# Final norm of the tokens spread over the last experts, and rows of the last three experts normed by themselves

## The chip, the cores and the metric

The kernel runs on one core of a Trainium2 chip. The metric is the device time of one execution in microseconds (us); for a kernel it is the median of several runs. A profile is one further execution, taken by the hardware profiler. Engines are named as in the profile: PE (matmul), PEld (its weight load), DVE (vector), ACT (scalar), POOL (GpSimd), SP (the queue that issues most DMAs).

## The reference

One layer over 1024 latent tokens of width 1024 and 256 context tokens: a token mixer, then a mixture of experts, then a final norm. What matters here is the end:

```python
def rmsnorm(x, g):
    y = x * lax.rsqrt(jnp.mean(x * x, axis=-1, keepdims=True) + EPS)
    return y * g

def expert_choice_ffn(h, w_r, w1, w3, w2):        # 16 experts, D 1024, F 2048
    cap = EC_FACTOR * n // N_EXPERTS               # 128 tokens for each expert
    aff = jax.nn.softmax(h @ w_r, axis=-1)
    gate, idx = lax.top_k(jnp.swapaxes(aff, 1, 2), cap)
    xe = h[bidx, idx]
    hid = jax.nn.silu(xe @ w1) * (xe @ w3)
    ye = (hid @ w2) * gate[..., None]
    return jnp.zeros_like(h).at[bidx, idx].add(ye)

x = x + g2x * expert_choice_ffn(hx2, w_router, w1, w3, w2)
return rmsnorm(x, final_g)
```

An expert chooses its 128 tokens, so a token may be chosen by several experts or by none, and a row of the output can be normed for good only when every expert that chose it has added its part. All data are fp32.

## The kernel before

The mixer, the second norm and the router take the time to about 480 us. They leave two arrays in DRAM: `hx2d`, the normed tokens that the experts gather from, and `x2d`, the residual stream that they add to. From there on the loop over 16 experts runs.

**One expert.** Its weights are 24 units of 1 MB, each 128 x 2048 fp32: eight of w1 and eight of w3 (up) and eight of w2 (down). SP loads them (`load_next`, L91) into a ring of 12 slots with the tag `raw`. A unit is split before use: ACT copies it rounded into `hi` (L107), DVE subtracts, `lo = raw - hi` (L109); three `hi`/`lo` pairs are held. PE then makes three passes over a unit (hi x hi, lo x hi, hi x lo: L1257, L1259, L1261 for up, L1300, L1303, L1306 for down). A slot of the ring comes free when DVE has made `lo`.

**Routing.** `route_oh(e)` makes on DVE a one-hot block `oh` (L1218) from the positions of the router. `route(e)` multiplies it on PE into the token numbers `ix` and the gates `gate` (L1226 to L1230) and gathers the expert's rows `xe` from `hx2d` with an indirect DMA that POOL issues (L1235). `transpose_x(e)` turns `xe` into its `hi` and `lo`. `oh` and `xe` share a tag `xe` with two buffers.

**Order.** Instructions run on each engine in the order in which the program writes them. The loop is software-pipelined by hand: iteration e runs `up("3", e)`, with `transpose_x(e+1)` behind its unit 2, `route_oh(e+2)` behind unit 3 and `route(e+2)` behind unit 6; then `hidden(e)` (DVE, L1278: the product of silu and the second up product, four pieces `sg`); `up("1", e+1)` with `transpose_h(e)` in it; and `down(e)` with the silu of expert e+1 in it (ACT, L1268). The last two iterations are in another order: up 3 of 14, up 1 of 15, silu, up 3 of 15, down of 14, down of 15.

**End of an expert.** At the end of `down(e)` DVE makes `ye`, the product of the PSUM result, the gate and the row `g2row` (L1313, two halves of 512), and POOL issues an indirect DMA that adds the 128 rows of `ye` into `x2d` (L1316, the scatter-add). `ye` has a buffer of its own in the pool `mb`.

**The end before.** Expert 15 has no scatter-add. SP reads `x2d` back in four pieces `xf` (L1384) once the scatter-add of expert 14 has landed. `ye` of expert 15 is split into `yh` and `yl` and spread by matmuls with the one-hot block `ohT` (L1374; L1403 to L1405) over the eight token tiles. For each tile: the sum (`residual`, DVE L1412, or within PSUM), Square and Sqrt on ACT (L1422, L1427), reciprocal on DVE (L1439), the product with the gain row `fg` (DVE L1446, or POOL L1434 and DVE L1444), and an output DMA by SP (L1447).

Of the kernel before, what the change touches and what calls it, by code (L numbers as in the profile page):

```python
# [45 lines left out]
def hybrid_layer(ctx, tc, x, c, ctxt, c_ctx, w_mod, b_mod, norm1_g, norm2_g, w_in, sgu_g, sgu_w,  # L46
# [36 lines left out]

    def load_next(n=1, queue=nc.sync):
        for _ in range(n):
# [1136 lines left out]
    def route(e):  # L1222
# [8 lines left out]
        if e == NE - 1:  # L1231
            V.tensor_copy(ixf, p[:, 0:1])
# [148 lines left out]
    xf = [raw2([P, 4, D], F32, "xf") for _ in range(2)]  # L1381
    fs = mp.tile([P, 3, 8], F32, name="fs")
    for q in range(4):
        nc.sync.dma_start(xf[q // 2][:, q % 2 * 2:q % 2 * 2 + 2],  # L1384
                          x2d[q * 256:(q + 1) * 256].rearrange("(t p) d -> p t d", p=P))
    ye = down(NE - 1)
    yh = mb.tile([P, D], F32R, name="yh", tag="xth")
    yl = mb.tile([P, D], F32R, name="yl", tag="xtl")
    for n in range(2):
# [1 line left out]
        A.activation(yh[:, sl], ye[:, sl], AF.Copy)
        V.tensor_sub(yl[:, sl], ye[:, sl], yh[:, sl])
    FP, XS = {}, {}

    def spread(t, add):

        v = xf[t // 4][:, t % 4]
        FP[t] = [bank([P, 512], "fp") for _ in range(2)]
        for n in range(2):
            sl = slice(n * 512, (n + 1) * 512)  # L1400
            p = FP[t][n]
            if add:
                PE.matmul(p, ident, v[:, sl], start=True, stop=False)  # L1403
            PE.matmul(p, ohT[:, t * P:(t + 1) * P], yh[:, sl], start=not add, stop=False)
            PE.matmul(p, ohT[:, t * P:(t + 1) * P], yl[:, sl], start=False, stop=True)  # L1405
        if add:
            XS[t] = FP[t]

    def residual(t):
        v = xf[t // 4][:, t % 4]  # L1410
        for n in range(2):
            V.tensor_add(v[:, n * 512:(n + 1) * 512], v[:, n * 512:(n + 1) * 512], FP[t][n])  # L1412
        XS[t] = [v]

    fo = {}

    def square(t):
# [92 lines left out]
```

## Time and profile before

| | us |
|---|---|
| median of 3 runs (1645.67 to 1648.39) | 1646.16 |
| profiled execution | 1644.65 |
| its span | 1642.6 |
| mean granted clock of TensorE, of full speed | 0.967 |

| engine | busy us | share of the span |
|---|---|---|
| PE | 1537.4 | 94% |
| DVE | 1385.6 | 84% |
| ACT | 1090.2 | 66% |
| POOL | 143.2 | 9% |

The DMA engines moved 485.30 MB, 295 GB/s over the span. The span is the time from the first to the last recorded event of the profiled execution; that execution's own time is 2.05 us longer. "Busy" leaves out the issuing of DMAs on SP. In rows of a timeline the first number is the start, the second the length from the first to the last of the instructions that the row merges; `[0.19 <-ACT hi L107]` at the end of a row means that the engine stood idle for 0.19 us before it and was released by that instruction.

### The profile page before, as it was taken

The page shows a single profiled execution, that of the slowest core. Times are in us where ns is not written, and L with a number is a line of the kernel's source. Part 1 is how long each engine was busy: PE and PEld are TensorE (multiplying, and loading weights), DVE is VectorE, ACT ScalarE, POOL GpSimd, SP SyncE. Part 2 cuts the span into 40 slices and gives each one's busy share as a digit, 9 for nine tenths or more (in the row PEclk, how much of TensorE's full clock was granted, in tenths as well). Part 3 has the DMA queues.
Part 4 walks back from the last instruction along what each step waited for, and adds up shares of the span by engine and source line. Part 5 has one row for each costly group of instructions (what it writes and reads, how often), then busy time and mean ns, then how long its engine had stood idle before and what let it go on. Part 6 is the DMA issues. An engine that isn't in the chain of part 4 may idle for free.

```text
span 1642.6 us, 19121 instructions
## 1 busy us (share of the span) xinstructions
PE 1537.4 (94%) x7288; PEld 1263.9 (77%) x7288; DVE 1385.6 (84%) x1321; ACT 1090.2 (66%) x990; POOL 143.2 (9%) x126
## 2 busy tenths in 40 slices
PE   5899997989939999999999999999999999999996
PEld 2687777878727888888888888888888888887784
DVE  6669687667875998989989899898988989898897
ACT  6576652632336778687777777768777786777873
POOL 2311121000000000100101000010000101001002
PEclk8999998999959999999999999999999999999998
DMA  9010147333566999999999999999999999999855
GB/s 383 28 36 29 65 154 253 134 128 116 214 268 239 366 384 385 376 360 387 381 373 391 367 378 369 388 383 378 371 364 388 380 382 381 357 388 382 317 188 205
DMA packets 85947, 485.30 MB, mean 295 GB/s; under 512 B 11224, under 2 KB 20064, under 8 KB 35680
## 3 DMA queue, kind: packets, MB, share of 16 engines
q1 hardware_dynamic: 80896, 466.72, 73.9%
q0 software_dynamic: 4864, 17.34, 4.1%
q8 instruction: 57, 0.93, 0.2%
q14 instruction: 34, 0.28, 0.0%
q10 hardware_dynamic: 96, 0.03, 0.0%
HBM read 463.61 MB, written 20.45 MB: 295 GB/s over the span
## 4 chain that ended last, share of the span: by engine, by line
PE 69%; DVE 13%; DMA 7%; ACT 7%; issue 4%; POOL 1%; SPq 0%; DVEq 0%; POOLq 0%; ACTq 0%
PE h L1257 11%; PE h L1261 11%; PE h L1259 11%; PE ye L1303 7%; PE ye L1300 7%; PE ye L1306 7%; DMA raw<-in_w_dram 3%; ACT hi L107 3%; DVE lo L109 3%; DMA ring<-in_w_mod_dram 2%; PE pw L931 2%; PE pw L933 2%; PE pw L935 2%; PE hp L1284 2%; DVE sg L1278 1%
## 5 line engine op out<-in xcount | busy, mean ns | idle before, releaser
L109 DVE TENSOR_TENSOR lo<-raw,hi 128x2048 fp32r<-128x2048 f32 x383 | 870.7, 2291 | 123.7 <-ACT hi L107 120.1
L107 ACT ACTIVATE hi<-raw 128x2048 fp32r<-128x2048 f32 x384 | 737.1, 1921 | 223.4 <-PE h L1261 158.2
L1257 PE MATMUL h<-hi,xth 128*128 128x512 f32 x1024 | 293.1, 400 | 3.6 <-ACT sg L1268 1.3
L1259 PE MATMUL h<-lo,xth 128*128 128x512 f32 x1024 | 280.3, 390 | 1.9 <-DVE lo L109 1.9
L1261 PE MATMUL h<-hi,xtl 128*128 128x512 f32 x1024 | 280.1, 390 | 0.0
L1257 PEld LDWEIGHTS h<-hi,xth 128*128 128x128 f32 x1024 | 188.1, 189 | 50.7 <-DVE sg L1278 12.5
L1259 PEld LDWEIGHTS h<-lo,xth 128*128 128x128 f32 x1024 | 192.7, 188 | 42.8 <-DVE lo L109 2.8
L1261 PEld LDWEIGHTS h<-hi,xtl 128*128 128x128 f32 x1024 | 192.6, 188 | 40.7
L1300 PE MATMUL ye<-hi,hth 128*128 128x512 f32 x512 | 157.9, 390 | 0.0
L1303 PE MATMUL ye<-lo,hth 128*128 128x512 f32 x512 | 157.8, 389 | 0.0
L1306 PE MATMUL ye<-hi,htl 128*128 128x512 f32 x512 | 157.7, 389 | 0.0
L1316 POOL DMA_INDIRECT x2d<-ye,ix x15 | 50.1, 3338 | 790.5 <-DVE ye L1313 790.5
L1306 PEld LDWEIGHTS ye<-hi,htl 128*128 128x128 f32 x512 | 96.1, 188 | 20.1
L1303 PEld LDWEIGHTS ye<-lo,hth 128*128 128x128 f32 x512 | 96.0, 188 | 20.2 <-DVE lo L109 0.3
L1300 PEld LDWEIGHTS ye<-hi,hth 128*128 128x128 f32 x512 | 95.8, 188 | 19.6
L1268 ACT ACTIVATE sg<-h 128x512 f32<-128x512 f32 x64 | 69.9, 1111 | 0.1
L1287 ACT ACTIVATE hth<-hp 128x512 fp32r<-128x512 f32 x64 | 35.0, 596 | 42.3 <-PE hp L1284 42.3
L404 DVE SCALAR_TENSOR_TENSOR ring<-ring,cs 128x1024 f32<-128x1024 f32 x28 | 41.4, 1479 | 14.0 <-DMA ring<-in_w_mod_dram 13.4
L377 PE MATMUL pu<-hxh,wh 128*128 128x512 f32 x128 | 50.8, 397 | 2.6 <-ACT g1row L738 2.6
L1235 POOL DMA_INDIRECT xe<-hx2d,ix x16 | 17.1, 1068 | 400.2 <-DVE gate L1230 238.5
L379 PE MATMUL pu<-hxl,wh 128*128 128x512 f32 x128 | 50.9, 398 | 0.0
L378 PE MATMUL pu<-hxh,wl 128*128 128x512 f32 x128 | 50.8, 397 | 0.0
(346 smaller groups left out, 1910.7 us busy)
## 6 DMA issues: line engine op xcount, KB each, us to landing
raw<-in_w_dram SPq DMA_DIRECT2D x383, 1024.0 KB, 7.3
ring<-in_w_mod_dram SPq DMA_DIRECT2D x32, 512.0 KB, 4.9
wmod<-in_w_mod_dram SPq DMA_DIRECT2D x8, 1024.0 KB, 10.5
wraw<-in_w_in_dram SPq DMA_DIRECT2D x6, 1024.0 KB, 12.1
xh<-in_x_dram SPq DMA_DIRECT2D x4, 1024.0 KB, 15.6
wor<-in_w_out_dram SPq DMA_DIRECT2D x4, 1024.0 KB, 7.8
xr<-in_x_dram SPq DMA_DIRECT2D x8, 512.0 KB, 4.2
x2d<-xr SPq DMA_DIRECT2D x8, 512.0 KB, 2.6
```

The source lines that it names most:

```text
L107: A.activation(hi, s, AF.Copy)
L109: eng.tensor_tensor(lo, s, hi, op=OP.subtract)
L377: PE.matmul(p, w[0][:, k], act[0][:, k], start=(k == 0), stop=False)
L378: PE.matmul(p, w[1][:, k], act[0][:, k], start=False, stop=False)
L379: PE.matmul(p, w[0][:, k], act[1][:, k], start=False, stop=(k == 7))
L1257: PE.matmul(pt[b], hi[:, k], wh[:, b * 512:(b + 1) * 512], start=(k == 0), stop=False)
L1259: PE.matmul(pt[b], hi[:, k], wl[:, b * 512:(b + 1) * 512], start=False, stop=False)
L1261: PE.matmul(pt[b], lo[:, k], wh[:, b * 512:(b + 1) * 512], start=False, stop=(k == 7))
L1268: A.activation(s.rearrange("t j p -> t p j"), pt[b].rearrange("t (p j) -> t p j", j=4), AF.Silu)
L1300: PE.matmul(pt[n], hi[:, j], wh[:, j2 * 1024 + n * 512:j2 * 1024 + n * 512 + 512], start=st_, stop=False)
L1303: PE.matmul(pt[n], hi[:, j], wl[:, j2 * 1024 + n * 512:j2 * 1024 + n * 512 + 512], start=False, stop=False)
L1306: PE.matmul(pt[n], lo[:, j], wh[:, j2 * 1024 + n * 512:j2 * 1024 + n * 512 + 512], start=False, stop=en)
```

## The change

- **Tiles normed early.** Eight tiles of 128 tokens, f0 to f7, are read from `x2d` by SP behind eight chosen weight loads (in up 3 of expert 14, up 1 and up 3 of expert 15), squared on ACT behind the weight unit of the same name, multiplied on DVE one unit later, and written to `out` by POOL. Their `x2d` holds the experts up to 12 (f0 to f3) or 13 (f4 to f7).
- **Rows of the last three experts again.** The rows of expert 13 (f8) and 14 (f9) are gathered from `x2d` once their scatter-adds have landed, normed, and scattered over the same rows of `out`, f8 and f9 within the two last downs. The rows of expert 15 (f10) are gathered, its `ye` is added to them at the end, and they are normed and scattered last. These scatters wait for the outputs before them.
- **No spread.** `ohT`, `yh`, `yl`, the matmuls of `spread`, `xf` and the split of work with POOL in the tail are gone.
- **Buffers.** `fn`, the tiles' buffers, take slots of the ring `raw`. `fg` is broadcast at the start of the experts and has its own buffer. `ye` leaves `mb` and takes the tag `xe` with its two buffers, beside `oh` and `xe`. Two pads move addresses.

```diff
@@ -81,6 +81,8 @@
     units, ready, pieces = [], {}, []
     nsplit, nused = [0], [0]
 
+    behind, at = {}, {}
+
     def load_next(n=1, queue=nc.sync):
         for _ in range(n):
             which, w, e, u = pieces.pop(0)
@@ -90,6 +92,7 @@
             src = w[e, q * P * r:(q + 1) * P * r, :].rearrange("(p k) f -> p (k f)", p=P)
             queue.dma_start(t, src[:, h * 2048:(h + 1) * 2048])
             units.append(((which, e, u), t))
+            behind.get((which, e, u), lambda: None)()
 
     def plan(which, w, e):
         pieces.extend((which, w, e, u) for u in range(8))
@@ -1207,6 +1210,7 @@
 
 
     mp = ctx.enter_context(tc.tile_pool(name="mp", bufs=1))
+    mp.tile([P, 16], F32, name="mp_pad")
     sxs = ExitStack()
     sx = sxs.enter_context(tc.tile_pool(name="sx", bufs=2))
     xe, ix, xT, sg, hT = {}, {}, {}, {}, {}
@@ -1228,8 +1232,6 @@
         g = mp.tile([P, 1], F32, name="gate", bufs=4)
         V.tensor_copy(i, p[:, 0:1])
         V.tensor_reduce(g, p[:, 1:3], axis=AX.X, op=OP.add)
-        if e == NE - 1:
-            V.tensor_copy(ixf, p[:, 0:1])
         ix[e] = (i, g)
         xe[e] = mp.tile([P, D], F32, name="xe", bufs=2)
         G.indirect_dma_start(out=xe[e], out_offset=None, in_=hx2d,
@@ -1261,6 +1263,8 @@
                     PE.matmul(pt[b], lo[:, k], wh[:, b * 512:(b + 1) * 512], start=False, stop=(k == 7))
             if k in mid:
                 mid[k]()
+            for f in at.get((which, e, k), ()):
+                f()
         return pt
 
     def silu1(e, pt, b):
@@ -1307,15 +1311,68 @@
                               start=False, stop=en)
             if u in mid:
                 mid[u]()
-        ye = mb.tile([P, D], F32, name="ye")
+            for f in at.get(("2", e, u), ()):
+                f()
         i, g = ix[e]
+        if e + 1 == NE:
+            return pt, g
+        ye = mp.tile([P, D], F32, name="ye", tag="xe", bufs=2)
         for n in range(2):
             V.scalar_tensor_tensor(ye[:, n * 512:(n + 1) * 512], pt[n], g, g2row[:, n * 512:(n + 1) * 512],
                                    op0=OP.mult, op1=OP.mult)
-        if e + 1 < NE:
-            G.indirect_dma_start(out=x2d, out_offset=bass.IndirectOffsetOnAxis(ap=i[:, :1], axis=0),
-                                 in_=ye, in_offset=None, compute_op=OP.add)
-        return ye
+        G.indirect_dma_start(out=x2d, out_offset=bass.IndirectOffsetOnAxis(ap=i[:, :1], axis=0),
+                             in_=ye, in_offset=None, compute_op=OP.add)
+
+
+    fs = mp.tile([P, 3, 12], F32, name="fs")
+    FN = {}
+
+    def f_slot(j):
+        FN[j] = raw([P, 2, D], F32, "fn")
+        return FN[j]
+
+    def f_load(j):
+        nc.sync.dma_start(f_slot(j)[:, 0], x2d[j * P:(j + 1) * P])
+
+    def f_gather(j, e):
+        G.indirect_dma_start(out=FN[j][:, 0], out_offset=None, in_=x2d,
+                             in_offset=bass.IndirectOffsetOnAxis(ap=ix[e][0][:, :1], axis=0))
+
+    def f_square(j):
+        A.activation(FN[j][:, 1], FN[j][:, 0], AF.Square, scale=1.0 / 32.0, accum_out=fs[:, 0, j:j + 1])
+        A.activation(fs[:, 2, j:j + 1], fs[:, 0, j:j + 1], AF.Sqrt, bias=epst)
+
+    def f_out(j, e=None):
+        V.reciprocal(fs[:, 2, j:j + 1], fs[:, 2, j:j + 1])
+        o = FN[j][:, 1]
+        V.scalar_tensor_tensor(o, FN[j][:, 0], fs[:, 2, j:j + 1], fg, op0=OP.mult, op1=OP.mult)
+        if e is None:
+            G.dma_start(out[j * P:(j + 1) * P], o)
+        else:
+            f_scatter(j, e)
+
+    def f_scatter(j, e):
+        G.indirect_dma_start(out=out, out_offset=bass.IndirectOffsetOnAxis(ap=ix[e][0][:, :1], axis=0),
+                             in_=FN[j][:, 1], in_offset=None)
+
+    def when(which, e, u, *fs_):
+        at.setdefault((which, e, u), []).extend(fs_)
+
+    spots = [("3", NE - 2, 1), ("3", NE - 2, 3), ("3", NE - 2, 5), ("3", NE - 2, 7),
+             ("1", NE - 1, 5), ("1", NE - 1, 7), ("3", NE - 1, 2), ("3", NE - 1, 4)]
+    nxt_ = {("3", NE - 2, 8): ("1", NE - 1, 0), ("1", NE - 1, 8): ("3", NE - 1, 0)}
+    for j, (w_, e_, u_) in enumerate(spots):
+        behind[w_, e_, u_] = lambda j=j: f_load(j)
+        when(w_, e_, u_, lambda j=j: f_square(j))
+        when(*nxt_.get((w_, e_, u_ + 1), (w_, e_, u_ + 1)), lambda j=j: f_out(j))
+
+    def again(j, e, *key):
+
+        f_slot(j)
+        f_gather(j, e)
+        which, e2, u = key
+        when(which, e2, u, lambda: f_square(j))
+        when(which, e2, u + 1, lambda: f_out(j, e))
 
     load_next(2)
     route_oh(0)
@@ -1333,16 +1390,19 @@
                                                   reuse_waits="tile"))
     g2row = mp.tile([P, D], F32, name="g2row")
     row_bcast(g2row, mcol[:, 3])
+    fg = mp.tile([P, D], F32, name="fg")
+    row_bcast(fg, fgc)
     transpose_x(0)
     p1 = up("1", 0, {1: lambda: route(1)})
     sxs.close()
     gap = ctx.enter_context(tc.tile_pool(name="gap", bufs=1))
-    gap.tile([P, 32], F32, name="gap_pad")
+    gap.tile([P, 64], F32, name="gap_pad")
     mb = ctx.enter_context(tc.tile_pool(name="mb", bufs=1))
     silu(0, p1)
-    ixf = mp.tile([P, 1], F32, name="ixf")
     for e in range(NE):
         nxt = e + 1 < NE
+        if e == NE - 1:
+            again(8, e - 2, "2", e - 1, 2)
         if nxt:
             load("1", w1, e + 1)
         if e < NE - 2:
@@ -1367,115 +1427,28 @@
             else:
                 silu(e + 1, p1)
         else:
-            A.preload_act_table_set("sqrt_and_others")
-            iw = mp.tile([P, S], F32, name="iw", tag="xe", bufs=2)
-            G.iota(iw, pattern=[[1, S]], base=0, channel_multiplier=0, allow_small_or_imprecise_dtypes=True)
-            ohT = mp.tile([P, S], F32R, name="ohT", tag="xth")
-            V.tensor_scalar(ohT, iw, ixf, None, op0=OP.is_equal)
-            fg = mp.tile([P, D], F32, name="fg", tag="xe", bufs=2)
-            row_bcast(fg, fgc)
             hidden(e, up("3", e, mid))
             down(e - 1, {u: lambda b=b: transpose_h(e, (b,)) for b, u in enumerate((1, 3, 5, 7))})
 
 
-    xf = [raw2([P, 4, D], F32, "xf") for _ in range(2)]
-    fs = mp.tile([P, 3, 8], F32, name="fs")
-    for q in range(4):
-        nc.sync.dma_start(xf[q // 2][:, q % 2 * 2:q % 2 * 2 + 2],
-                          x2d[q * 256:(q + 1) * 256].rearrange("(t p) d -> p t d", p=P))
-    ye = down(NE - 1)
...
+    again(9, NE - 2, "2", NE - 1, 5)
+    f_slot(10)
+    f_gather(10, NE - 1)
+    pt, g = down(NE - 1)
+    x, o = FN[10][:, 0], FN[10][:, 1]
     for n in range(2):
         sl = slice(n * 512, (n + 1) * 512)
...
+        V.scalar_tensor_tensor(o[:, sl], pt[n], g, g2row[:, sl], op0=OP.mult, op1=OP.mult)
+        V.tensor_add(x[:, sl], x[:, sl], o[:, sl])
+        A.activation(o[:, sl], x[:, sl], AF.Square, scale=1.0 / 32.0, accum_out=fs[:, n, 10:11])
+        if n == 0:
+            A.activation(fs[:, 0, 10:11], fs[:, 0, 10:11], AF.Identity, bias=epst)
+    A.activation(fs[:, 2, 10:11], fs[:, 1, 10:11], AF.Sqrt, bias=fs[:, 0, 10:11])
+    V.reciprocal(fs[:, 2, 10:11], fs[:, 2, 10:11])
+    for n in range(2):
+        sl = slice(n * 512, (n + 1) * 512)
+        V.scalar_tensor_tensor(o[:, sl], x[:, sl], fs[:, 2, 10:11], fg[:, sl], op0=OP.mult, op1=OP.mult)
+    f_scatter(10, NE - 1)
 
 
 # ---- launch: one core; inputs and outputs as the reference has them ----
```

**The order on DVE around `oh`.** Rows of the engine in program order, with the semaphores that each waits for (`DMASW` are those of DMAs that POOL issues, `DMAHW` those of SP). Before, from `ye` of expert 12 to `oh` of expert 15 in `up("3", 13)`:

```order
L1313 SCALAR_TENSOR_TENSOR ye<-ye,gate,g2row 128x512 [waits DMASW2_49,PE_49]
L1313 SCALAR_TENSOR_TENSOR ye<-ye,gate,g2row 128x512 [waits PE_49]
L109 TENSOR_TENSOR lo<-raw,hi 128x2048 [waits DMAHW1_49,Activation_49]
L109 TENSOR_TENSOR lo<-raw,hi 128x2048 [waits DMAHW2_49,Activation_49]
L109 TENSOR_TENSOR lo<-raw,hi 128x2048 [waits DMAHW3_49,Activation_49]
L1247 TENSOR_TENSOR xtl<-xp,xth 128x512 [waits Activation_49] x2
L109 TENSOR_TENSOR lo<-raw,hi 128x2048 [waits DMAHW4_49,Activation_49]
L1218 TENSOR_TENSOR oh<-iota_s,pos 128x1024
L109 TENSOR_TENSOR lo<-raw,hi 128x2048 [waits DMAHW5_49,Activation_49]
L109 TENSOR_TENSOR lo<-raw,hi 128x2048 [waits DMAHW6_49,Activation_49]
L109 TENSOR_TENSOR lo<-raw,hi 128x2048 [waits DMAHW7_49,Activation_49]
```

The same place of the change:

```order
L1321 SCALAR_TENSOR_TENSOR ye<-ye,gate,g2row 128x512 [waits PE_49] x2
L112 TENSOR_TENSOR lo<-raw,hi 128x2048 [waits DMAHW1_49,Activation_49]
L112 TENSOR_TENSOR lo<-raw,hi 128x2048 [waits DMAHW2_49,Activation_49]
L112 TENSOR_TENSOR lo<-raw,hi 128x2048 [waits DMAHW3_49,Activation_49]
L1249 TENSOR_TENSOR xtl<-xp,xth 128x512 [waits Activation_49] x2
L112 TENSOR_TENSOR lo<-raw,hi 128x2048 [waits DMAHW4_49,Activation_49]
L1222 TENSOR_TENSOR oh<-iota_s,pos 128x1024 [waits DMASW4_49]
L112 TENSOR_TENSOR lo<-raw,hi 128x2048 [waits DMAHW5_49,Activation_49]
L112 TENSOR_TENSOR lo<-raw,hi 128x2048 [waits DMAHW6_49,Activation_49]
L112 TENSOR_TENSOR lo<-raw,hi 128x2048 [waits DMAHW7_49,Activation_49]
```

The instructions stand in the same order. `ye` waited for a `DMASW` semaphore and waits only for PE; `oh` waited for none and waits for `DMASW4`. This is the last of 13 such places.

**The order on DVE in up 3 of expert 15.** Before, from `ohT` on:

```order
L1374 TENSOR_SCALAR ohT<-iw,ixf 128x1024 [waits Pool_49]
L109 TENSOR_TENSOR lo<-raw,hi 128x2048 [waits DMAHW1_49,PE_49,Activation_49]
L109 TENSOR_TENSOR lo<-raw,hi 128x2048 [waits DMAHW2_49,Activation_49]
L109 TENSOR_TENSOR lo<-raw,hi 128x2048 [waits DMAHW3_49,Activation_49]
L109 TENSOR_TENSOR lo<-raw,hi 128x2048 [waits DMAHW4_49,Activation_49]
L109 TENSOR_TENSOR lo<-raw,hi 128x2048 [waits DMAHW5_49,Activation_49]
```

The same stretch of the change (`fn` are the tiles f5, f6 and f7):

```order
L1346 RECIPROCAL fs<-fs 128x1
L1348 SCALAR_TENSOR_TENSOR fn<-fn,fs,fg 128x1024 [waits DMAHW4_49,DMASW0_49,DVE_49]
L112 TENSOR_TENSOR lo<-raw,hi 128x2048 [waits DMAHW1_49,Activation_49]
L112 TENSOR_TENSOR lo<-raw,hi 128x2048 [waits DMAHW2_49,Activation_49]
L112 TENSOR_TENSOR lo<-raw,hi 128x2048 [waits DMAHW4_49,Activation_49]
L1346 RECIPROCAL fs<-fs 128x1
L1348 SCALAR_TENSOR_TENSOR fn<-fn,fs,fg 128x1024 [waits DMAHW0_49,DVE_49]
L112 TENSOR_TENSOR lo<-raw,hi 128x2048 [waits DMAHW5_49,Activation_49]
L112 TENSOR_TENSOR lo<-raw,hi 128x2048 [waits DMAHW6_49,Activation_49]
L1346 RECIPROCAL fs<-fs 128x1
L1348 SCALAR_TENSOR_TENSOR fn<-fn,fs,fg 128x1024 [waits DMAHW3_49,DVE_49]
```

`ohT` is gone; a reciprocal and a product of 128x1024 now stand behind every second or third unit (f5's are the first).

**The order on POOL at the end.** Before:

```order
L1316 DMA x2d<-ye,ix 1024x1024
L1235 DMA xe<-hx2d,ix 128x1024
L1316 DMA x2d<-ye,ix 1024x1024
L1372 IOTA iw 128x1024
L1316 DMA x2d<-ye,ix 1024x1024
L1434 TENSOR_TENSOR fo<-xf,fg 128x1024 x4
```

The change:

```order
L1237 DMA xe<-hx2d,ix 128x1024
L1323 DMA x2d<-ye,ix 1024x1024
L1350 DMA out_dram<-fn 128x1024 x5
L1338 DMA fn<-x2d,ix 128x1024
L1350 DMA out_dram<-fn 128x1024 x3
L1355 DMA out_dram<-fn,ix 1024x1024
L1323 DMA x2d<-ye,ix 1024x1024
L1338 DMA fn<-x2d,ix 128x1024 x2
L1355 DMA out_dram<-fn,ix 1024x1024 x2
```

The multiplies and the iota are gone; eight output DMAs, three gathers (`fn<-x2d,ix`) and three scatters (`out_dram<-fn,ix`) have come.

## Rows read from the trace of the kernel before

**Rows 1.** windows, two stretches: engines' busy us (instructions), granted clock, DMA share, GB/s.
```profile
585.00:1440.00 855.00, 853.83 (x3936) 705.58 (x3935) 774.32 (x481) 642.02 (x418) 55.16 (x25) 1.00 0.99 377
...
1543.00:1612.00 69.00, 66.84 (x298) 53.99 (x297) 56.67 (x34) 46.69 (x31) 3.35 (x1) 1.00 0.65 237
```

**Rows 2.** timeline of DVE, one expert: start us, us, instruction, count, [idle].
```profile
1356.05 6.92 DVE L109 TENSOR_TENSOR lo<-raw,hi 128x2048 fp32r<-128x2048 f32 x3
...
1367.02 1.22 DVE L1218 TENSOR_TENSOR oh<-iota_s,pos 128x1024 fp32r<-128x1024 f32 x1
1368.15 6.69 DVE L109 TENSOR_TENSOR lo<-raw,hi 128x2048 fp32r<-128x2048 f32 x3
...
1375.17 2.34 DVE L109 TENSOR_TENSOR lo<-raw,hi 128x2048 fp32r<-128x2048 f32 x1 [0.19 <-ACT hi L107]
1377.43 2.47 DVE L1278 TENSOR_TENSOR sg<-sg,h 128x512 f32<-128x512 f32 x4
```

**Rows 3.** timeline of PE, the same expert: around the first unit of up 1.
```profile
1370.30 1.07 PE L1257 MATMUL h<-hi,xth 128*128 128x512 f32 x4
...
1373.02 0.95 PE L1226 MATMUL pr<-tvr,oh 128*128 128x4 f32 x8
...
1377.15 0.62 PE L1259 MATMUL h<-lo,xth 128*128 128x512 f32 x2
...
1378.16 1.09 PE L1257 MATMUL h<-hi,xth 128*128 128x512 f32 x2
```

**Rows 4.** timeline of POOL, the same expert.
```profile
1356.41 3.37 POOL L1316 DMA_INDIRECT x2d<-ye,ix  x1 [49.81 <-DVE ye L1313]
1375.18 0.98 POOL L1235 DMA_INDIRECT xe<-hx2d,ix  x1 [15.40 <-DVE gate L1230]
```

**Rows 5.** line L1316, landing: 13 scatter-adds (585 to 1450 us); the last.
```profile
DMA to landing us min/median/max: 11.6/14.1/14.9
...
DMA to landing us min/median/max: 7.9/7.9/7.9
```

**Rows 6.** line L404, whole span: duration in ns, min/median/max.
```profile
L404 DVE SCALAR_TENSOR_TENSOR ring<-ring,cs x28: 1277/1285/3847, 205.9 to 311.8; 128x1024 f32<-128x1024 f32 x28
```

**Rows 7.** timeline of DVE, the tail.
```profile
1611.04 1.41 DVE L1313 SCALAR_TENSOR_TENSOR ye<-ye,gate,g2row 128x512 f32<-128x512 f32 x2 [3.69 <-PE ye L1306]
...
1613.77 2.54 DVE L1412 TENSOR_TENSOR xf<-xf,fp 128x512 f32<-128x512 f32 x4
1616.66 0.16 DVE L1439 RECIPROCAL fs<-fs 128x1 f32<-128x1 f32 x1 [0.35 <-ACT fs L1427]
1616.86 3.36 DVE L1446 SCALAR_TENSOR_TENSOR fo<-xf,fs,fg 128x1024 f32<-128x1024 f32 x1
```

**Rows 8.** timeline of ACT, the tail.
```profile
1615.14 1.06 ACT L1422 ACTIVATE fo<-xf 128x1024 f32<-128x1024 f32 x1 [2.04 <-DVE xf L1412]
1616.11 0.18 ACT L1422 ACTIVATION_READ_ACCUMULATOR fo<-xf 128x1 f32 x1
1616.33 0.30 ACT L1427 ACTIVATE fs<-fs,epst 128x1 f32<-128x1 f32 x1
...
1617.90 0.58 ACT L1422 ACTIVATE fo<-fp 128x512 f32<-128x512 f32 x1
```

**Rows 9.** timeline of ACT, the table load before the last expert.
```profile
1543.34 1.28 ACT L1370 ACT_TABLE_LOAD   x1
1544.63 1.09 ACT L738 ACTIVATE fg<-rb 128x512 f32<-128x512 f32 x2
```

**Rows 10.** waits of the DMA queue SP, 1390 to 1643 us: us, times, longest.
```profile
SPq L91 <- DVE lo L109: 159.3, 62, 7.8
```

**Rows 11.** line L1235, 400 to 500 us: waited for the gather (us, times).
```profile
  PE xp L1245: 7.3, 1
```

**Rows 12.** line L1447, the output DMAs: issue ns, first and last start; landing.
```profile
L1447 SPq DMA_DIRECT2D out_dram<-fo x8: 332/332/351, 1620.2 to 1638.4; - x8
...
DMA to landing us min/median/max: 2.6/2.6/3.0
```

More of the change, by code (lines that the diff above doesn't have):

```diff
@@ L1378, in hybrid_layer @@
             down(e - 1, {u: lambda b=b: transpose_h(e, (b,)) for b, u in enumerate((1, 3, 5, 7))})
-    xf = [raw2([P, 4, D], F32, "xf") for _ in range(2)]
-    fs = mp.tile([P, 3, 8], F32, name="fs")
-    for q in range(4):
-        nc.sync.dma_start(xf[q // 2][:, q % 2 * 2:q % 2 * 2 + 2],
-                          x2d[q * 256:(q + 1) * 256].rearrange("(t p) d -> p t d", p=P))
-    ye = down(NE - 1)
-    yh = mb.tile([P, D], F32R, name="yh", tag="xth")
-    yl = mb.tile([P, D], F32R, name="yl", tag="xtl")
+    again(9, NE - 2, "2", NE - 1, 5)
@@ L1389, in hybrid_layer @@
+    f_slot(10)
+    f_gather(10, NE - 1)
+    pt, g = down(NE - 1)
+    x, o = FN[10][:, 0], FN[10][:, 1]
     for n in range(2):
         sl = slice(n * 512, (n + 1) * 512)
[L1391 to L1417, printed above, removed]
-        if t not in fo:
-            fo[t] = raw([P, 2, D], F32, "fo")
-        w = D // len(XS[t])
-        for n, v in enumerate(XS[t]):
-            A.activation(fo[t][:, 1, n * w:(n + 1) * w], v, AF.Square, accum_out=fs[:, n, t:t + 1])
-        m = epst
-        if len(XS[t]) > 1:
-            m = fs[:, 0, t:t + 1]
-            A.activation(m, m, AF.Identity, bias=epst, scale=1.0 / D)
-        A.activation(fs[:, 2, t:t + 1], fs[:, len(XS[t]) - 1, t:t + 1], AF.Sqrt, bias=m, scale=1.0 / D)
@@ L1429, in hybrid_layer @@
-    GM = set()
-    def gains(t):
-        fo[t] = raw([P, 2, D], F32, "fo")
-        G.tensor_tensor(fo[t][:, 0], XS[t][0], fg, op=OP.mult)
-        GM.add(t)
-    def finish(t):
-        o, r = fo[t][:, 0], fs[:, 2, t:t + 1]
-        V.reciprocal(r, r)
-        w = D // len(XS[t])
-        for n, v in enumerate(XS[t]):
-            sl = slice(n * w, (n + 1) * w)
-            if t in GM:
-                V.tensor_scalar(o, o, r, None, op0=OP.mult)
-            else:
-                V.scalar_tensor_tensor(o[:, sl], v, r, fg[:, sl], op0=OP.mult, op1=OP.mult)
-        nc.sync.dma_start(out[t * P:(t + 1) * P], o)
@@ L1449, in hybrid_layer @@
-    for t, add in ((0, False), (1, False), (5, False), (2, True), (3, True)):
-        spread(t, add)
-    residual(0)
-    square(0)
-    residual(1)
-    gains(1)
-    square(1)
-    finish(0)
-    residual(5)
-    gains(5)
-    spread(6, False)
-    spread(7, False)
-    square(2)
-    finish(1)
-    square(5)
-    finish(2)
-    spread(4, True)
-    residual(6)
-    gains(6)
-    square(3)
-    finish(5)
-    finish(3)
-    square(6)
-    residual(7)
-    gains(7)
-    finish(6)
-    square(4)
@@ L1476, in hybrid_layer @@
-    finish(4)
-    square(7)
-    finish(7)
+        V.scalar_tensor_tensor(o[:, sl], pt[n], g, g2row[:, sl], op0=OP.mult, op1=OP.mult)
[5 more added lines that the diff above has]
+    V.reciprocal(fs[:, 2, 10:11], fs[:, 2, 10:11])
```

## The prediction

> **What bounds the kernel now.** I read the windows first, to see which engine has room in which stretch. From the second expert to the fifteenth (585 to 1440 us) PE is busy 853.8 of 855.0 us at a granted clock of 1.00, DVE 774.3 and the DMA engines 0.99 of the time [rows 1]: PE sets the pace, and anything that makes PE wait there is added whole. From 1543 to 1612 us DVE is busy 56.7 of 69 us and DMA 0.65, so there is some room [rows 1]; behind 1611.04 comes the tail, DVE's chain of residual, norm and output [rows 7]. Then DVE's timeline in one ordinary expert [rows 2]: from the one-hot `oh` at 1367.02 to the product `sg` of `hidden` at 1377.43 it stands still only 0.19 us. PE's timeline shows why that matters [rows 3]: the two matmuls at 1378.16 take 1.09 us where the two at 1377.15 take 0.62, because the bank that they start on is read by `hidden` until then. So in each expert PE's path runs once through DVE, and a stall of DVE between `oh` and `hidden` reaches PE nearly one for one.
>
> **The wait on `oh`.** The diff gives `ye` the tag of `xe`. There are two buffers under it, and in the order of allocation `ye` of an expert comes into the one that the next `oh` overwrites. The order on DVE says the same: `oh` waited for nothing and now waits for a DMASW semaphore, that of the scatter-add that reads `ye`. Before, `ye` had a buffer to itself and only the next `ye`, an expert period later, waited for that landing. `route_oh(e+2)` runs in `up("3", e)`, after the scatter-add of expert e-1, for e = 1 to 13: 13 waits.
> The price is landing time against the place of `oh`. The scatter-add starts on POOL at 1356.41 [rows 4], `oh` on DVE at 1367.02 [rows 2]: 10.6 us later, and nothing between the two moves. The scatter-adds of these 13 experts land 11.6 us after their start at the least, 14.1 in the median, 14.9 at the most [rows 5]. So none of the 13 has landed when `oh` comes up. Behind it stand three `lo`, `ix`, `gate`, another `lo` and `hidden`, which PE waits for; 0.2 us of the stall goes into the gap of 0.19 [rows 2]. With a landing of L, the loss for each expert is L - 10.6 - 0.2. The ends are 13 x 0.8 = 10 us (all at 11.6) and 13 x 4.1 = 53 us (all at 14.9). I take 13.5, under the median, since an expert period that is some 3 us longer moves the same bytes and leaves the scatter-add a little less to share with: 13 x 2.7 = **+35 us**. Each us of landing is worth 13 us of the result, which makes this the widest term.
> Here a rule speaks the other way. The row says 11.6 to 14.9 us for this transfer of 128 rows of 4 KB [rows 5]. The Trainium skill ("DMA: Bandwidth & Descriptors", section Anatomy of one DMA, SWDGE path) fits a DMA issued by GpSimd with about 2.0 us plus its bytes over 436 GB/s; for 512 KB my estimate from it is 3.2 us, `oh` would find the buffer free, and the sum would be 35 us less. The trace does not agree, so the sum goes by the rows; what the kernel would do without the wait is the first rival.
>
> **The norms among the last experts.** Ten tiles (f0 to f7 whole, f8 and f9 gathered) are now normed before the last matmul. A 128x1024 product of this kind takes 1.285 us on DVE [rows 6] and the reciprocal 0.16 [rows 7]: 1.45 us for a tile. They stand mostly one to two weight units. A unit takes PE 2.72 us, from the start of its first pass at 1370.30 to 1373.02 [rows 3], and DVE 6.69 / 3 = 2.23 us for its `lo` in a row, 2.3 by itself [rows 2], 2.29 taken; so two units and a tile are 2 x 2.29 + 1.45 = 6.03 us on DVE against 5.44 on PE, 0.59 us too much. Ten times that is 5.9 us. On ACT a tile is 1.06 + 0.18 + 0.30 = 1.5 us [rows 8]; with two `hi` it stays within the room that ACT has (46.7 busy of 69 us, [rows 1]), so I cost it at nothing, and if that room were gone it would be as many us again. The square root now comes between two uses of silu: two table loads more, of 1.28 us as the one before [rows 9], while the copy of `fg` (1.09 us, [rows 9]) leaves this place; I put half of the difference of 1.5 on the path: 0.7. Together **+6.6 us**. Ends: 0, since DVE has 12 us idle in 1543 to 1612 [rows 1], and 10 x 1.45 + 2.6 = 17, with nothing hidden.
> By the Trainium skill ("ScalarE: Activation LUTs", What ACT_TABLE_LOAD costs) each switch is 1.28 us and a drain of 1.38 behind it. The row shows the 1.28 and the next instruction 1.29 after its start, so the trace has no drain there; by the page the sum would be up to 2.8 us more.
> **Loads and queues.** SP issues eight loads of `x2d` more between the weight loads, and the tiles sit in slots of the weight ring, so a weight is loaded later than now. SP waits 159.3 us of the last 253 for slots that DVE frees [rows 10]: slots pace the loads, and the transfers hide behind the DMA's free 0.35 of 69 us [rows 1]. Cost nothing; without this cover it is the third rival. POOL gets eight output issues and the gathers and scatters; nothing but outputs stands behind them. The broadcast of `fg` at the start lies where PE waits 7.3 us for the gather of the first `xe` [rows 11]: nothing, or at most about 1 us without that wait.
>
> **The tail.** Now the first `ye` product starts at 1611.04 [rows 7] and the span ends at 1642.6: 31.6 us. After the change, what follows the last matmul is: product and sum of two halves, 1.41 for the two products and half of the 2.54 of four sums, 2.7 us [rows 7]; the Square of the second half and its accumulator, 0.58 + 0.18, and the Sqrt, 0.30 [rows 8], 1.1; reciprocal 0.2 [rows 7]; two half products, together as long as a whole one, 1.3 [rows 6]; five crossings between engines at some 0.1: 5.8 us in all. Then the scatter, for which no row stands without accumulation: issue between 0.98 (the gather) and 3.37 us (the scatter-add) [rows 4]; I take 1.0, as it only copies, like the gather. Landing between 2.6 us (plain outputs, [rows 12]) and 7.9 - 3.4 = 4.5 (the last scatter-add without its issue, [rows 4, 5]); I take 3.6. The last output now is issued at 1638.4 and lands 2.6 later, at 1641.0 [rows 12], which leaves 1.6 for the close. Sum 5.8 + 1.0 + 3.6 + 1.6 = 12: **-19.6 us**, with ends at 11 and 17 (the dear issue, and the scatter of f9 landing late, which this one waits for).
>
> **The sum.** 1642.6 + 35.1 + 6.6 - 19.6 = 1664.7 us of span. The profiled execution has 2.05 us around its span, which gives 1666.7; it is 1.5 us under the median of the runs shown. I forecast **1667 us**.
>
> **Rivals.**
> *The scatter-add lands before `oh`.* Then there is no wait: 1666.7 - 35.1 = 1632 us, faster. For it: the scatter-add of expert 14, with little else moving, lands after 7.9 us [rows 5]. Against: in the steady stretch the DMA engines are 0.99 busy [rows 1], and none of the 13 landed under 11.6. It decides at a landing of 10.8 us, at 13 us for each us. I give it 0.13. Between it and the forecast, at landings near 12, lies a result of about 1646, as now: 0.04.
> *DVE slows beside POOL.* One product of this form took 3.36 us beside a POOL multiply [rows 7], 2.07 more than the usual 1.285. If POOL's output issues did the same to all ten, it would be 21 us: 1688. Against: three `lo` beside the scatter-add took 6.92 us, without it 6.69 [rows 2]. 0.05.
> *Late weights.* Tiles, gathers and early outputs put about 7 MB more ahead of the last matmul (16 transfers of 0.5 MB for f0 to f7, five for f8 to f10, less the 4 MB of `x2d` that are read there now), at 377 GB/s [rows 1] 18 us of transfers. If none of it were hidden: 1685. Against: 0.35 x 69 = 24 us of the DMA are free. 0.08.
>
> **How the numbers follow.** The forecast has 0.70. About 0.2% (3.3 us) is what a measurement of this kernel can tell from no change. Faster is the first rival alone, 0.13; the same is 0.04; slower is the forecast and the two dear rivals, 0.83. The range 1645 to 1685 leaves out the first rival and about 0.06 above; it holds landings from about 11.8 to 14.9 with the other terms as taken.
>
> **What would show it.** Right: DVE idle before `oh`, 1 to 4 us each, 35 to 41 in all, released by the landing of `x2d`; scatter-adds about 72.3 us apart instead of 69.5; PE idle by as much; three table loads among the last experts; 12 us from the last down matmul to the end. Wrong: `oh` with no idle ahead of it and the expert period unchanged (first rival); long products beside POOL's issues; PE waits on `lo` that go back to a landing of `raw`; or a tail well over 17 us.

## The result and the profile after

| | before | after |
|---|---|---|
| median, us | 1645.91 (4 runs) | 1684.64 (4 runs, 1673.55 to 1687.18) |
| profiled execution, its span | 1644.65, 1642.6 | 1684.14, 1682.4 |
| PE busy | 1537.4 (94%) | 1562.3 (93%) |
| DVE busy | 1385.6 (84%) | 1377.6 (82%) |
| POOL busy | 143.2 (9%) | 169.0 (10%) |

The change is slower: the ratio to the kernel before is 1.0229, 95% interval 1.0203 to 1.0256, that is 38 us. The forecast was 1667 us, slower by 21; the sign and the main mechanism were right, the size was not, and the measured time stands at the upper end of the range.

The wait that was forecast is there. The line of `oh` in the changed kernel, with what DVE stood idle for ahead of it (us, times), and the landing of the 13 scatter-adds (us after their start), which answers to [rows 5]:

```profile
L1222 DVE TENSOR_TENSOR oh<-iota_s,pos x16: 1219/1226/1227, 479.9 to 1485.4; 128x1024 fp32r<-128x1024 f32 x16
...
its engine sat idle before it (us, times) until:
  DMA x2d<-ye,ix: 27.8, 13
```

```profile
L1323 POOL DMA_INDIRECT x2d<-ye,ix x13: 3367/3381/3421, 594.9 to 1472.3; - x13
...
DMA to landing us min/median/max: 11.7/12.8/14.7
```

All 13 `oh` wait, 27.8 us in all; the forecast had 2.9 each (before 0.2 of gap is taken off), the trace has 2.1. In one expert, DVE's timeline (which answers to [rows 2]):

```profile
1114.11 2.29 DVE L112 TENSOR_TENSOR lo<-raw,hi 128x2048 fp32r<-128x2048 f32 x1 [0.72 <-ACT hi L110]
1118.94 1.23 DVE L1222 TENSOR_TENSOR oh<-iota_s,pos 128x1024 fp32r<-128x1024 f32 x1 [2.54 <-DMA x2d<-ye,ix]
1120.08 6.69 DVE L112 TENSOR_TENSOR lo<-raw,hi 128x2048 fp32r<-128x2048 f32 x3
...
1129.02 2.47 DVE L1282 TENSOR_TENSOR sg<-sg,h 128x512 f32<-128x512 f32 x4
```

The scatter-add of this expert starts at 1105.39. DVE is ready for `oh` at 1116.40, 11.0 us later, and gets it at 1118.94, when the landing releases it. The three `lo` and `sg` move back by as much.

PE in the same expert (answers to [rows 3]) shows the wait reaching it, and something that was not in the forecast:

```profile
1117.03 1.09 PE L1259 MATMUL h<-hi,xth 128*128 128x512 f32 x4
1117.96 1.09 PE L1261 MATMUL h<-lo,xth 128*128 128x512 f32 x4
1118.89 1.09 PE L1263 MATMUL h<-hi,xtl 128*128 128x512 f32 x4
1119.83 1.09 PE L1259 MATMUL h<-hi,xth 128*128 128x512 f32 x4
1122.42 1.20 PE L1261 MATMUL h<-lo,xth 128*128 128x512 f32 x4 [1.50 <-DVE lo L112]
```

PE waits 1.50 us for the first `lo` behind `oh`. But ahead of that wait, where nothing is late, its passes already start 0.93 us apart: a unit of three passes takes from 1117.03 to 1119.83, 2.80 us, where it took 2.72 before. This is so in all experts: the median distance from one matmul of 512 columns to the next is 227 ns before and 234 after, in up and in down, while the transposes of `sg` (109 ns) and three groups of matmuls of the same size in the mixer (226, 229 and 232 ns) are unchanged. The granted clock is no cause: it is 1.00 in most experts, and 0.99 in the window that answers to [rows 1]:

```profile
585.00:1440.00 855.00, 839.10 (x3746) 672.37 (x3745) 737.82 (x460) 611.30 (x398) 71.02 (x24) 0.99 0.97 360
```

So the steady stretch has two losses: the wait, and slower matmuls. The expert period went from 69.5 to 73.1 us (12 periods between the first and the thirteenth scatter-add, 594.9 to 1472.3), 3.6 us longer; DVE's idle before `oh` is 2.1 us of an expert.

The end went as forecast. DVE's first product behind the last matmul, and POOL's last scatter:

```profile
1670.09 0.75 DVE L1441 SCALAR_TENSOR_TENSOR fn<-ye,gate,g2row 128x512 f32<-128x512 f32 x1 [2.32 <-PE ye L1310]
```

```profile
1675.96 0.98 POOL L1355 DMA_INDIRECT out_dram<-fn,ix  x1 [6.94 <-DVE fn L1450]
```

From 1670.09 to the end of the span at 1682.4 it is 12.3 us, against 31.6 before [rows 7] and 12 in the forecast. The scatter was issued in 0.98 us, like the gather, not in 3.4, and the one before it landed 3.4 us after its start.

### The profile page after: what moved, and what is told of

Same layout as the page of the kernel before. It is cut to its first block, busy times and chain, and to the rows that moved or that the text cites. A ratio compares the mean times of both kernels' runs of the same rounds, so it can differ in the third digit from the quotient of the medians.

```text
span 1682.4 us, 19023 instructions
## 1 busy us (share of the span) xinstructions
PE 1562.3 (93%) x7244; PEld 1259.9 (75%) x7244; DVE 1377.6 (82%) x1313; ACT 1096.7 (65%) x993; POOL 169.0 (10%) x135
## 5 line engine op out<-in xcount | busy, mean ns | idle before, releaser
L1259 PE MATMUL h<-hi,xth 128*128 128x512 f32 x1024 | 299.1, 406 | 8.0 <-DVE sg L1282 2.9
L1261 PE MATMUL h<-lo,xth 128*128 128x512 f32 x1024 | 290.0, 400 | 16.1 <-DVE lo L112 16.1
L1263 PE MATMUL h<-hi,xtl 128*128 128x512 f32 x1024 | 288.1, 398 | 0.0
L1237 POOL DMA_INDIRECT xe<-hx2d,ix x16 | 37.6, 2347 | 434.2 <-DVE gate L1234 286.7
L1272 ACT ACTIVATE sg<-h 128x512 f32<-128x512 f32 x64 | 69.5, 1105 | 0.0
L407 DVE SCALAR_TENSOR_TENSOR ring<-ring,cs 128x1024 f32<-128x1024 f32 x28 | 41.9, 1495 | 14.0 <-DMA ring<-in_w_mod_dram 13.4
## 6 DMA issues: line engine op xcount, KB each, us to landing
wmod<-in_w_mod_dram SPq DMA_DIRECT2D x8, 1024.0 KB, 10.7
```

The lines of the kernel that those rows point to most:

```text
L1259: PE.matmul(pt[b], hi[:, k], wh[:, b * 512:(b + 1) * 512], start=(k == 0), stop=False)
L1261: PE.matmul(pt[b], hi[:, k], wl[:, b * 512:(b + 1) * 512], start=False, stop=False)
L1263: PE.matmul(pt[b], lo[:, k], wh[:, b * 512:(b + 1) * 512], start=False, stop=(k == 7))
L1272: A.activation(s.rearrange("t j p -> t p j"), pt[b].rearrange("t (p j) -> t p j", j=4), AF.Silu)
```

## The experiments

Ratios are to runs of the kernel before on the same chip; with 1646 us they are turned into us.

**1. The addresses alone, taken back.** In the changed kernel `xth`, `xtl`, `hth`, `htl`, `sg` and `oh` start 32 bytes off a multiple of 64; before, all started at multiples of 64. `hi`, `lo` and the ring did not move.

```diff
-    mp.tile([P, 16], F32, name="mp_pad")
+    mp.tile([P, 24], F32, name="mp_pad")
```

> The changed kernel with the first pad 32 bytes longer, so that the tiles behind it (xth, xtl, sg, hth, htl, oh, xe) start at multiples of 64 bytes again, as before the change; now they start 32 bytes off. Theory 1 (these addresses slow the matmuls: a pass of four takes 0.934 us in the changed kernel, 0.907 before): passes fall back to 0.907 us, 384 units x 3 passes x 0.027 = 31 us less, some 1653 us. Theory 2 (the passes are slower because of the stalls, the traffic or the chip, not the addresses): passes stay at 0.934 and the time at 1684 us.

Measured: 1679.92 us, ratio 1.0215 (1.0170 to 1.0261). The passes did fall back (227 ns from matmul to matmul), and the time hardly moved. The idle ahead of `oh`, and PE's line that waits for `lo` (the page's line: busy us, mean ns, idle before it and its releaser), show where it went:

```profile
  DMA x2d<-ye,ix: 38.7, 13
```

```profile
L1261 PE MATMUL h<-lo,xth 128*128 128x512 f32 x1024 | 288.2, 399 | 31.7 <-DVE lo L112 31.6
```

The wait grew from 27.8 to 38.7 us. With faster passes DVE is ready for `oh` 10.7 instead of 11.0 us after the start of the scatter-add, and the 13 landings came at 13.6 us on average instead of 13.1: 13 x 0.8 = 10 us, the difference. That is half of what was won: PE's busy time in an expert at full clock went from 71.5 to 69.8 us, 22 us in 13 experts. The clock took the other half. Six of the 13 experts have a granted clock under 1.00 here, and PE's busy time in them is together 15.4 us longer than at 69.8 each; in the changed kernel there are two, with 3.8 us. The longest of the six in this run (the last number but two is the granted clock):

```profile
879.09:956.06 76.97, 73.25 (x322) 60.52 (x321) 63.25 (x40) 52.24 (x35) 4.35 (x2) 0.93 0.93 343
```

The theory of the addresses was right on the passes and wrong on the time, since it left out that the wait, and the clock behind it, take back what PE wins.

**2. The addresses alone, added.** The kernel before with a pad:

```diff
     mp = ctx.enter_context(tc.tile_pool(name="mp", bufs=1))
+    mp.tile([P, 8], F32, name="mp_pad")
```

> The kernel before with one pad of 32 bytes ahead of the same tiles and nothing else. Theory 1: passes of 0.934 us in place of 0.907, some 31 us more, 1677 us. Theory 2: 1646 us, passes unchanged.

Measured: 1670.40 us, ratio 1.0152 (1.0123 to 1.0181), 25 us slower with no other change. PE's lines on its page (busy us, mean ns), which read 400, 390 and 390 ns before:

```profile
L1258 PE MATMUL h<-hi,xth 128*128 128x512 f32 x1024 | 297.8, 404 | 3.3 <-ACT sg L1269 1.1
L1260 PE MATMUL h<-lo,xth 128*128 128x512 f32 x1024 | 286.1, 396 | 1.8 <-DVE lo L109 1.8
L1262 PE MATMUL h<-hi,xtl 128*128 128x512 f32 x1024 | 286.2, 396 | 0.0
```

The distance of the matmuls is 235 ns. 32 bytes in the address cost 1.5% of the kernel.

**3. The wait alone, added.** The kernel before with `ye` under the shared tag:

```diff
-        ye = mb.tile([P, D], F32, name="ye")
+        ye = mp.tile([P, D], F32, name="ye", tag="xe", bufs=2) if e + 1 < NE else mb.tile([P, D], F32, name="ye")
```

> The kernel before with ye of experts 0 to 14 under the tag xe, as in the change, all other addresses unchanged: the wait of oh for the landing of the scatter-add alone. The theory of the prediction: DVE idle 28 to 41 us in all before oh in 13 waits, and as much more time, 1672 to 1687 us; passes stay at 0.907 by theory 1, and rise to 0.934 if stalls are what slows them (theory 2), then over 1700 us. Rival: the wait is made up elsewhere in the expert, and the time stays near 1646 us.

Measured: 1700.61 us, ratio 1.0333 (1.0298 to 1.0367), 55 us slower, with passes at 0.907 us: more than the 41 us that DVE stood idle. Idle of DVE ahead of `oh` in the 13 waits, then PE's wait for the `lo` behind it (us, times, longest):

```profile
  DMA x2d<-ye,ix: 41.2, 13
```

```profile
PE h L1259 <- DVE lo L109: 28.7, 12, 3.5
```

The rest is the clock. PE's timeline around one such wait:

```profile
1414.43 1.07 PE L1257 MATMUL h<-hi,xth 128*128 128x512 f32 x4
1418.82 1.32 PE L1259 MATMUL h<-lo,xth 128*128 128x512 f32 x4 [3.32 <-DVE lo L109]
1419.93 1.91 PE L1261 MATMUL h<-hi,xtl 128*128 128x512 f32 x4
...
1423.20 2.05 PE L1257 MATMUL h<-hi,xth 128*128 128x512 f32 x4
...
1426.68 1.08 PE L1261 MATMUL h<-hi,xtl 128*128 128x512 f32 x4
```

and four windows of this run (two of 3 us around this wait, then two whole experts; the last number but two is the granted clock):

```profile
1412.00:1415.00 3.00, 3.00 (x15) 2.50 (x14) 0.00 (x0) 2.20 (x2) 0.00 (x0) 1.00 1.01 406
1421.00:1424.00 3.00, 3.00 (x12) 2.72 (x12) 2.57 (x4) 1.91 (x1) 0.19 (x1) 0.50 0.97 385
666.89:738.10 71.21, 69.84 (x321) 57.28 (x321) 62.92 (x40) 52.24 (x35) 6.21 (x2) 1.00 0.98 366
1400.52:1476.31 75.79, 72.47 (x321) 59.91 (x321) 63.30 (x40) 52.23 (x35) 4.35 (x3) 0.95 0.94 347
```

PE idles 3.32 us; behind it the passes take twice as long, at a granted clock of 0.50 (the lower level, 1.2 GHz) from 1421 to 1424, and are back at the higher one by 1426.68. PE's busy time in that expert is 72.47 us, 2.6 more than in the expert that begins at 666.89, where PE waited 1.1 us and the clock stayed at 1.00. Seven of the 13 experts show a clock under 1.00 and are together 14.4 us longer in PE's busy time. In the six others the period grew by DVE's idle less 0.2 us, within 0.03: in the one that begins at 666.89, DVE idles 1.86 us and the expert takes 71.21 us, where 69.55 is usual. 41.2 - 13 x 0.2 + 14.4 = 53 us, which is the measured loss but for 2.

**4. The wait alone, taken away.** `oh` later in the changed kernel, behind the landing:

```diff
-            mid[3] = lambda: route_oh(e + 2)
+            mid[5] = lambda: route_oh(e + 2)
```

> The changed kernel with route_oh behind unit 5 of up 3 instead of unit 3: oh comes about 5.4 us later, behind the landing of the scatter-add, so its wait goes; addresses stay. The theory of the prediction: DVE no longer idle before oh, 28 us or a little more less, 1650 to 1657 us, with passes still at 0.934 by theory 1 (by theory 2 they fall to 0.907 and the time to about 1625). Rival: oh so late delays the matmul of route behind unit 6, and less than half of it is gained.

Measured: 1657.09 us, ratio 1.0072 (1.0047 to 1.0097). `oh` waits for nothing, the clock is 1.00 throughout the steady stretch, and the passes stay at 234 ns. 26 us are gained.

**5. Both taken away.** The edits of 1 and 4 together.

> The changed kernel with both edits: the first pad 32 bytes longer (passes back to 0.907 us) and route_oh behind unit 5 (no wait of oh). If the two effects are all that made the change slow, what is left is the gain of the shorter tail less the norms: the kernel of the run with oh at 5 was 11 us over before with slow passes, which cost the kernel before 24 us, so 1646 + 11 - 24 = 1633 us, 1628 to 1638, faster than before. Rival: with faster passes the loads or DVE bind in the last experts, and it stays at 1640 to 1650.

Measured: 1633.67 us, ratio 0.9945 (0.9924 to 0.9965), 9 us faster than before. The first `ye` product of the last expert in this run:

```profile
1620.35 0.75 DVE L1441 SCALAR_TENSOR_TENSOR fn<-ye,gate,g2row 128x512 f32<-128x512 f32 x1 [1.88 <-PE ye L1310]
```

The span ends at 1632.6, 12.3 us later. What is left of the change is its gain at the end, less the norms and some 3 us that the later `oh` costs (run 8).

**6. Which tiles.** As 5, with the second pad longer, so that only the pool `mb` is off:

```diff
-    gap.tile([P, 64], F32, name="gap_pad")
+    gap.tile([P, 72], F32, name="gap_pad")
```

> As the run before, with the second pad 32 bytes longer too: the tiles in mp (xth and xtl of even experts) start at multiples of 64 bytes, those in mb (xth and xtl of odd experts, hth, htl, sg) 32 bytes off. If the address of the stationary tile sets the pace of its own matmuls: passes of even up at 0.907 us, of odd up and of all downs at 0.934; two thirds of the 24 us, some 1633 + 16 = 1649 us. Rival (any tile off slows all, or only one pool counts): all passes alike, 1633 or 1657 us.

Measured: 1651.28 us, ratio 1.0042 (1.0027 to 1.0057), 16 us over run 5. A unit of PE in up 3 of expert 13 (`xth` in `mb`), then one in up 1 of expert 14 (`xth` in `mp`):

```profile
1443.16 1.10 PE L1259 MATMUL h<-hi,xth 128*128 128x512 f32 x4
...
1445.96 1.10 PE L1259 MATMUL h<-hi,xth 128*128 128x512 f32 x4
...
1467.85 1.07 PE L1259 MATMUL h<-hi,xth 128*128 128x512 f32 x4
...
1470.58 1.07 PE L1259 MATMUL h<-hi,xth 128*128 128x512 f32 x4
```

2.80 us against 2.73 us, and all downs have 235 ns from matmul to matmul. Each matmul pays for the address of its own stationary tile: that of its moving tile (`hi`, `lo`) is the same in both.

**7. A shorter wait.** The edit of 3, with `route_oh` behind unit 4.

> The kernel before with ye under the tag xe and route_oh behind unit 4 instead of 3: the wait is shorter by one unit, 2.7 us. With the landings of the run with oh at 3 (12.5 to 15.0 us after the start of the scatter-add) DVE would stand idle 0 to 1.7 us in an expert, 9 us in all. If the dear part of that run came from the clock, which fell to half after PE had been idle for 3.0 us or more: no granted clock under 0.97 in the steady stretch, each us of DVE idle costs 0.8 to 1.0 us, 1653 to 1656 us. Rival (a wait costs 1.3 us for each us whatever its length): 1658 us or more, clock unchanged.

Measured: 1658.50 us, ratio 1.0081 (1.0062 to 1.0101). This run does not decide what it was meant to decide. The landings were later than in run 3, so that DVE idled 14.9 us instead of 9, in 11 experts, and 13 us were lost, 0.9 for each. But the clock fell here too, in three experts, behind shorter waits. DVE's idle ahead of `oh` in all waits, and PE in one expert:

```profile
  DMA x2d<-ye,ix: 14.9, 11
```

```profile
1038.45 1.23 PE L1257 MATMUL h<-hi,xth 128*128 128x512 f32 x2 [1.44 <-DVE sg L1278]
1039.47 1.05 PE L1259 MATMUL h<-lo,xth 128*128 128x512 f32 x2
1040.32 1.05 PE L1261 MATMUL h<-hi,xtl 128*128 128x512 f32 x2
...
1042.80 1.08 PE L1259 MATMUL h<-lo,xth 128*128 128x512 f32 x4
```

A wait of PE of 1.44 us, and the next passes of two take 0.85 us from start to start instead of 0.45. In other experts of this run PE waited 1.7 us and kept the clock. That the fall belongs to waits of 3.0 us and more, as was expected, is wrong (in run 3 too it came behind one of 2.0 us); what decides it stays open.

**8. Is the later place free?** The edit of 4 in the kernel before.

> The kernel before with route_oh behind unit 5 and nothing else. If the later place of oh is free: 1644 to 1648 us, so that the run of the change with oh at 5 measures the wait alone. Rival: route, behind unit 6, now waits for oh and PE with it: 1.2 us for each of 14 experts, 1660 us.

Measured: 1647.76 us, ratio 1.0020 (1.0006 to 1.0033). About 3 us: the period is 69.74 us instead of 69.55. So the wait is worth 26 + 3 = 29 us in run 4.

**9. Those 3 us.** Run 5 with `route` behind unit 7.

> The changed kernel with both edits and route behind unit 7 instead of 6, so that its matmul no longer comes upon an oh that is still being made. The expert period was 69.74 us with oh at 5 against 69.55 before; if that 0.2 us is route's wait for oh, 14 experts give 2.7 us back: 1629 to 1632 us. Rival: ix and the gather come later and something else waits as long: 1633 us or more.

Measured: 1635.45 us, ratio 0.9943 (0.9928 to 0.9959), no better than run 5. The period is 69.88 us; PE now waits elsewhere (us, times, longest):

```profile
PE h L1259 <- DVE sg L1282: 2.9, 12, 0.3
```

The rival holds: `ix` and `gate` come right ahead of `hidden` on DVE, and PE waits for that.

**10. The norms.** Run 5 without f0 to f7, a kernel that leaves out the rows of the output which only these write.

> The changed kernel with both edits and without the eight tiles f0 to f7: their loads, squares, products and outputs are left out (only the rows of the last three experts are written). By the prediction's count they cost 8 x 0.59 + 0.7 = 5.4 us on the path: 1628 us. From the trace of the run with oh at 5, where the stretch from the scatter-add of expert 13 to the last matmul grew by 8.9 us of which 4 come from the slow passes, the ten tiles cost 5 us and these eight 4: 1630 us. Rival (they are hidden): 1633 to 1634 us.

Measured: 1629.77 us, ratio 0.9912 (0.9895 to 0.9929), 5 us under run 5. From the start of the scatter-add of expert 13 to the end of the last matmul it takes 114.6 us, in run 5 121.6, before 115.7. So the eight tiles cost 7.0 us there; some of it comes back in this run's tail, in which the product of f9 stands ahead of the last expert's and is late. All ten tiles, with what left that stretch, cost 121.6 - 115.7 = 5.9 us. PE's waits in that stretch of run 5 (us, times, longest):

```profile
PE h L1259 <- DVE sg L1282: 2.9, 1, 2.9
PE h L1261 <- DVE lo L112: 2.3, 3, 0.9
PE h L1259 <- ACT sg L1272: 2.1, 2, 1.7
PE ye L1307 <- DVE lo L112: 0.9, 2, 0.6
```

Before they were 0.9 for the `sg` of DVE, 0.5 for that of ACT and 1.1 for `lo`. So the loss is about a third each: `lo` that comes late, `hidden` that comes late, and a silu that comes late. Ahead of that silu ACT has, in run 5, a tile's Square and Sqrt and a table load, from 1546.31 to 1549.07.

## Why the prediction was right, and where it was off

**The wait on `oh`** is shown by runs 3 and 4: it is there, it is for the landing, and it was the larger part. Forecast 35 us; measured 26 in the changed kernel, where DVE idles 27.8 us (run 4), or 29 with the 3 us of run 8, and 55 in the kernel before (run 3). The formula L - 10.6 - 0.2 held in run 3, to 0.1 us, wherever the clock stayed at 1.00. Three errors of size are in this term. The first, the later arrival of `oh`, is a consequence of the slower passes: 11.0 us in place of "10.6 us later, and nothing between the two moves". The landing was 13.1 us on average and 13.5 had been taken; the reason given for a shorter landing, the longer expert period, did not hold in run 3, where the period is 73.4 us and the landings average 13.8, as before the change. And a us of idle was priced at one us, "nearly one for one"; the clock makes it 1.3 in run 3. In the changed kernel two experts have a clock under 1.00 (0.98 and 0.96), and their PE is 3.8 us longer. Run 1 is the change as the prediction had it in mind, with the addresses of before: its idle of 38.7 us is what was forecast (35 to 41), and most of what it is over 1667 us, at 1680, is the clock's 15 us, for which the sum has no term.

**The step that failed is one that the sum does not have.** The section on the change says that two pads move addresses, and the sum gives that no term and no bounds. It is worth 25 us by itself (run 2), about as much as the wait. No row of before could have priced it, since there `xth`, `xtl`, `hth` and `htl` all lie at multiples of 64 bytes; it needed a bound. That the measured 1684.6 us lies inside the range, 0.4 us under its upper end, is luck: that end was made of landings of 14.9 us, where they were 13.1, and held no room for the addresses. The Trainium skill ("SBUF — State Buffer", Operand start alignment) asks that an operand start at a multiple of its element size, and says of its own runs that they were on what is legal and timed nothing. The runs here are on the time: both addresses are legal, and they differ by 3% in each matmul.

**The norms**: forecast +6.6, measured +5.9 (run 5 against before). The size was right, the way there only in part: the sum laid nearly all of it on DVE's `lo`, ten times 0.59, and had ACT's tiles at nothing; but of what PE's waits grew by (run 10) a third is for `lo`. The eight whole tiles alone cost 7.0 us where 8 x 0.59 + 0.7 = 5.4 had been counted, and what left the stretch makes up for it. **The tail**: forecast -19.6, measured 12.3 - 31.6 = -19.3. Together -13.4 against -13.0. With the 3 us of the later `oh` that leaves -10, the difference of the spans of run 5 and of before (1632.6 and 1642.6).

**The sum.** -13.4 + 25 + 29 = 41 us, 38 measured. The two losses are not independent. With the wait in place the better addresses win 2 us in the ratio (1.0229 to 1.0215, which the intervals do not tell from nothing), without it 21 (1.0072 to 0.9945). Of the 47 us between run 5 and the change, the wait that is left alone keeps 44 (run 1), the addresses that are left alone 21 (run 4).

**The rivals.** That the scatter-add lands before `oh` is refuted: 11.7 us at the least. The estimate of 3.2 us that went with it is contradicted by the one landing with little else moving, 7.9 us in both kernels; the two last scatters of the change, of the same size but without the addition, landed 3.3 and 3.4 us after their start. DVE beside POOL's issues: the products of 128x1024 of the tiles took 1.28 to 1.29 us in the changed kernel, so no; but no output issue of POOL fell beside one of them, and only one ran beside a POOL instruction at all, the gather of f8 (1.285 us). Late weights: PE's waits for `lo` in the last experts come to 1.5 us in all behind 1500 us, so no.

## What to carry to other kernels

When a tile is given another's buffer, look at what the next owner now waits for, and set the landing of a DMA against the place of that owner on its engine; if it comes earlier, move it behind the landing before anything else. When tiles move, compare the distance of two matmuls in an undisturbed stretch before reading any wait: an address 32 bytes off a multiple of 64 under the stationary tile costs 3% there, and a pad takes it back. And measure two suspected losses both alone and together, since undoing one alone may show almost nothing (run 1).

## What the runs showed of the hardware

- A matmul of 128x512 in fp32r takes 227 ns from start to start with its stationary tile at a multiple of 64 bytes, 234 to 235 ns 32 bytes off it (runs 1, 2, 6), and no other offset was run; transposes of 128x128 by the identity keep 109 ns, although `sg` moved as well.
- The granted clock fell to 0.50 behind seven waits of PE of 2.0 to 3.5 us in run 3, while one of 2.6 us kept it; in run 7 it fell behind three of 1.4 to 1.7 us, and others of 1.7 kept it. The length of the wait does not decide it alone, and what else does is open. The fall added 1.3 to 3.5 us to PE's busy time in its expert (runs 1 and 3).
- A gather's issue on POOL took 0.98 us before and 2.85 in most experts after, with no price, as nothing waits for it there. The rows of POOL and of DVE in one expert after:

```profile
1127.11 2.85 POOL L1237 DMA_INDIRECT xe<-hx2d,ix  x1 [18.34 <-DVE gate L1234]
```

```profile
1126.82 2.28 DVE L112 TENSOR_TENSOR lo<-raw,hi 128x2048 fp32r<-128x2048 f32 x1
```

  The gather starts 0.29 us behind a `lo` and ends 0.86 us behind that one's end; before, it started within 0.01 us of it [rows 2, 4]. The Trainium skill ("SBUF — State Buffer", Who interferes with whom) says that a DVE instruction with two inputs in SBUF and a GpSimd instruction that reads SBUF exclude each other, and the first to start holds the port. These rows agree with it, and so does run 3, where the order changes from expert to expert: gathers that start ahead of a `lo` take 0.96 to 0.98 us, those that start 0.13 to 0.29 us behind one take 2.85 to 3.02 us and end 0.85 to 0.88 us behind its end. No run sets out to test it.
